# Step sizes on VectorE among the splits of X, a state-space product four pieces later in each head, meta tokens last in X, and q, k, v copied in destination order

## The chip, the cores and the metric

One core of a Trainium2 chip runs the whole layer in one launch. The metric is the device time of that launch in microseconds (us), from a run without the profiler; the trace comes from one further execution with it. PE is the matrix engine, PEld its weight loads, DVE the vector engine, ACT the scalar engine, POOL the general-purpose engine, SP the engine that issues most DMAs.

## The reference

The layer works on 16 meta tokens and 512 real tokens, 2048 channels wide, in float32. What is computed, cut to what matters here:

```python
proj = hf @ w_in                                  # 528 x 2048 by 2048 x 6144
u_ssm, g_ssm, q, k, v, g_sb = split(proj)         # each 1024 wide
# state-space branch: 64 groups of 16 channels, 64 complex states
dt = exp(log_dt); mag = exp(lam_re * dt); angle = lam_im * dt
h_t = (mag * e^{i angle}) * h_{t-1} + B u_t ;  y = Re(C h) + d * u
y_ssm = (GLU(gelu(y)) * silu(g_ssm)) @ w_branch_ssm
# stick-breaking attention, 8 heads of 128, strictly causal, scores q k / sqrt(128)
y_sb = (attention(q, k, v) * silu(g_sb)) @ w_branch_sb
gates = sigmoid(hf @ w_gate + b_gate)
out = layer_norm(ALPHA * hf + (gates_1 * y_ssm + gates_2 * y_sb) @ w_out)[16:]
```

## The kernel before, in words

Every float32 matrix product is done as three products of halves: an operand `a` is split into `ah` (rounded to the matrix engine's format by an ACT copy) and `al` (the rest, a DVE subtraction, `split_lo`, line 96), and `mm3` adds `ah*bh + ah*bl + al*bh`. The transposed input X is kept split in SBUF, `Xh` and `Xl`, as 16 chunks of 128 channels (`split_x`). The weights stream in from memory as 238 chunks of 128x1024 (`raw`), which ACT and DVE split into `whi` and `wlo` (`prep_upto`, line 126 and again line 96), three buffers each.

PE's work is cut into **pieces**. A unit of work is one output tile of 128 channels: 16 pieces, one for each chunk of X, 8 pieces for each weight chunk (a **slot**). `unit_real` multiplies the 512 real tokens (3 products of 512 columns in a piece), `unit_full` all 528 in two halves of 272 and 256 columns, `HALF` (6 products in a piece), `unit_pair`, used once at the start for u and v of head 0, two outputs at a time (12 products in a piece). A unit's result leaves the accumulator in a `fin_...` function at the start of the next slot.

The order of everything is the order in which the program is written: each engine takes its instructions in that order, and an instruction that waits holds up all behind it on its engine. Work beside the weight products is placed by hand: `schedule` takes pairs of a piece number and a function, counted from the piece at hand, and `run_fillers` calls each function just ahead of its piece. So a **step at piece 34** stands, on every engine that it uses, between the instructions of pieces 33 and 34.

The stages that the change touches:
- **Parameters** (start of the program, pieces 0 to 63). `params_a` computes the step sizes dt = exp(log_dt) and from them `mag` and `th`, on POOL; `params_v` (sine, cosine, exponential on DVE, in small steps), `params_g` (power tables on POOL) and `params_w` (further tables on DVE, ending in `pvt`, which `store_pv` writes to memory) follow. `steps(g, at, end, n)` spreads a generator's steps over the pieces from `at` to `end`.
- **Splits of X.** During the pair of units at the start, X's chunk c is split two pieces ahead of the piece that needs it.
- **Head stages** (`ssm_stages(i)` and `att_stages(i)`), which run while PE does the 80 weight pieces of the next head. In the state-space part, `s2` builds the tile `ot` on DVE, `s3` multiplies it with `bb` (8 small products, line 702), `s3b` takes the result out (ACT copy, DVE addition of `dd`, a DMA to `sd`), `s4` loads it back as `mt`, `s5` (line 731) starts the scan that `s7` ends. `s3` and `s5` write the same PSUM tile, aux2, of which there is one. In the attention part, `zblk` and `zb` make scores and a scan, `t01` and `t0` transpose the weights, `evb` splits the transposed tile (`ath` by ACT, `atl` by DVE), and `av(0)` at piece 37 multiplies them with the values `vh`, `vl`. `f3` of head 0 (six DVE operations, `ec` and `es`) stands at piece 46.

Meta tokens have columns 0 to 15 of X, real tokens 16 to 527. The real tokens are stored time step by time step (j) within blocks (k), so q, k and v are put into natural order by the copy that takes them out of PSUM.

Of the kernel before, what the change touches and what calls it, by code (L numbers as in the profile page):

```python
# [12 lines left out]
ALU = mybir.AluOpType  # L13
# [6 lines left out]
T = 8  # L20
NK = 66
MK = 2
L = T * NK
S = 512
SK = S // T
NM = T * MK
HALF = ((0, 272), (272, L))
LP = 576
NT = 8
NG = 8  # L30
# [8 lines left out]
def kernel(  # L39
# [49 lines left out]
    for kind, _ in MIX_ORDER:  # L89
        n_ = 4 if kind == "g" else 2  # L90
# [4 lines left out]
    def tt(out, a, b, op, eng=V):  # L95
        eng.tensor_tensor(out, a, b, op)  # L96

    def split_lo(lo, src, hi):
        tt(lo, src, hi.bitcast(F32), ALU.subtract)
# [31 lines left out]
    def mm3(o, ah, al, bh, bl, start, stop):  # L131
        PE.matmul(o, ah, bh, start=start, stop=False)  # L132
        PE.matmul(o, ah, bl, start=False, stop=False)  # L133
        PE.matmul(o, al, bh, start=False, stop=stop)  # L134
# [25 lines left out]
    def schedule(items):  # L160
        fillers.extend((piece[0] + p_, f) for p_, f in items)
        fillers.sort(key=lambda t: t[0])
# [20 lines left out]
    with tc.manual_schedule():  # L183
# [21 lines left out]
        def split_x(c):  # L205
            x, n = xts[c]
            r = x[:, 0, :].rearrange("p (j k) -> p j k", k=NK)[:, :, MK:NK]
            h, lo = jk(Xh[:, c, NM:L], SK), jk(Xl[:, c, NM:L], SK)
            A.copy(h, r)
            if n:  # L210
                m = x.rearrange("p c (j k) -> p c j k", k=NK)[:, :, :, 0:MK]
                mh_, ml_ = (t[:, c:c + n, 0:NM].rearrange("p c (j k) -> p c j k", k=MK) for t in (Xh, Xl))
                A.copy(mh_, m)
            split_lo(lo, r, h)
            if n:
                split_lo(ml_, m, mh_)
# [61 lines left out]
        def ts(o, a, s1, s2, op0, op1, e=V):  # L278
            e.tensor_scalar(o, a, s1, s2, op0, op1)
# [181 lines left out]
        zer = tp.tile([16, 112], F32, name="zer")  # L461

        def params_a():
            yield from vexp(dt, dt, G, "g")
            tt(mag, lr, dt, ALU.mult, G)
            tt(th, li, dt, ALU.mult, G)

        def params_v():

# [9 lines left out]
        def params_g():  # L479
            tt(mg8, mag[:, 0:64], mag[:, 0:64], ALU.mult, G)  # L480
            tt(mg8, mg8, mg8, ALU.mult, G)
            tt(mg8, mg8, mg8, ALU.mult, G)
            yield from params_e()
# [71 lines left out]
        def drain(g):  # L555
            for _ in g:
                pass
# [8 lines left out]
        def steps(g, at, end, n):  # L566
            def one_(g=g):
                next(g, None)
            return [(at + ((end - at) * k) // n, one_) for k in range(n)] + [(end, lambda: drain(g))]
# [4 lines left out]
        def store_pv():  # L574
            for src, dst in pvt_:
# [2 lines left out]
            [(18, lambda: [SP.dma_start(out=sd[i].rearrange("c (g t) -> c g t", t=240)[:, :, 0:112],  # L578
                                            in_=zer[:, None, :].to_broadcast([16, NG, 112]))
                           for i in range(NT)])]  # L580
            + [(2, lambda: drain(params_a())), (3, lambda: ts(maskl, masku, -1.0, 1.0, ALU.mult, ALU.add, G))]
            + steps(gv_, 19, 35, 40)
            + [(35, lambda: drain(params_g()))]
            + steps(gw_, 35, 60, 37)
            + [(61, store_pv)]
        )

        mp = None
# [61 lines left out]
        def ssm_stages(i):  # L650
# [143 lines left out]
                    in_=z.rearrange("p g k -> p (g k)"),  # L794
                )

            a = [(13, s1), (16, s1b), (20, s2(0)), (24, s2(1)), (26, s2(2)), (34, s3), (36, s3b), (39, s4)]
            if i == 0:
                a = [(24, s1), (27, s1b), (29, s2(0)), (31, s2(1)), (33, s2(2)), (37, s3), (39, s3b), (42, s4)]
            return [(0, s0)] + a + [  # L800
                (50, s5), (52, s5a), (55, s5b), (57, s5c), (66, s7), (69, s7b), (71, s8), (74, s9)]

# [152 lines left out]
        def unit_real(finish):  # L955
            a = new_acc()
            for half in range(2):
                def mk(kk, half=half):
                    def f(h, lo):
                        c = 8 * half + kk  # L960
                        ws = slice(kk * P, (kk + 1) * P)
                        mm3(a, h[:, ws], lo[:, ws], Xh[:, c, NM:L], Xl[:, c, NM:L],
                            c == 0, c == KT - 1)
                    return f
                slot([mk(kk) for kk in range(8)], (lambda: finish(a)) if half else None)


        def parts(t, aa):
            n = t[:, NM:L].rearrange("p (k j) -> p j k", j=T)
            yield n[:, 0:4, :], jk(aa[0][:, NM:272], SK)  # L970
            yield n[:, 4:8, :], jk(aa[1][:, 0:256], SK)
            yield t[:, 0:NM].rearrange("p (k j) -> p j k", j=T), jk(aa[0][:, 0:NM], MK)


        late = [lambda c=c: split_x(c) for c in range(1, KT)]
# [25 lines left out]
        for i in range(NT):  # L1001
            def fin_u(aa, i=i):
                u = ta("us", [P, L])
                uj = jk(u, NK)[:, ::-1, :]
                A.copy(uj[:, 0:4, MK:NK], jk(aa[0][:, NM:272], SK))
                A.copy(uj[:, 4:8, MK:NK], jk(aa[1][:, 0:256], SK))
                A.copy(uj[:, :, 0:MK], jk(aa[0][:, 0:NM], MK))
                A.dma_start(out=ud[i], in_=u)

            def fin_g(a, i=i):  # L1010
                t = ta("gsig", [P, S])
                A.activation(t, a, ACTF.Sigmoid)
                g_ = ta("gs", [P, S], F32, 2)
                tt(g_, a, t, ALU.mult)
                heads.setdefault(i, {})["gs"] = g_

            def fin_v(aa, i=i):
                v = ta("vT", [P, L])
                for d, a in parts(v, aa):
                    A.copy(d, a)  # L1020
                heads.setdefault(i, {})["vT"] = v

            def fin_k(aa, i=i):
                kh, kl = ta("kh", [P, L], F32R), ta("kl", [P, L], F32R)
                for (d, a), (l_, _) in zip(parts(kh, aa), parts(kl, aa)):
                    A.copy(d, a)
                    split_lo(l_, a, d)
                heads[i]["kh"], heads[i]["kl"] = kh, kl

            def fin_q(a, i=i):  # L1030
                qh, ql = ta("qh", [P, S], F32R), ta("ql", [P, S], F32R)
                A.copy(nat(qh), jk(a, SK))
                split_lo(nat(ql), jk(a, SK), nat(qh))
                heads[i]["qh"], heads[i]["ql"] = qh, ql

            if i == 0:
                unit_pair(fin_u, fin_v)
                unit_real(fin_g)
            else:
                unit_full(fin_u)  # L1040
                unit_real(fin_g)
                unit_full(fin_v)
            unit_full(fin_k)
            unit_real(fin_q)
            run_fillers()
            assert not fillers, fillers
            if i == 0:
                mb_st, at = open_main()
                f1, f2, f3 = ssm_load(0)
                schedule([(3, f2), (4, f1), (46, f3), (17, lambda: [V.tensor_copy(a[:, 4, 0:128], d0[:, 0:2, 0:64]) for a in at])])  # L1050
            schedule(ssm_stages(i) + att_stages(i))
            if i < NT - 1:
                f1, f2, f3 = ssm_load(i + 1)
                schedule([(45, f1), (61, f3), (72, f2)])


        def fin_gs(a, j):
# [206 lines left out]
        c = ctr[0]  # L1264
# [115 lines left out]
```

## Time and profile before

| what | us |
|---|---|
| time, median of 3 runs (1495.54 to 1496.41) | 1495.86 |
| time of the profiled execution | 1495.39 |
| its span, first to last instruction | 1493.6 |
| around the span in that execution (the difference) | 1.8 |
| PE busy with matmuls | 1454.4 (97%) |
| DVE busy | 764.9 (51%) |
| ACT busy | 421.3 (28%) |
| POOL busy | 68.6 (5%) |

Busy time is the sum of an engine's instruction durations with overlaps counted once. PE is close to full over the whole span, so what is left of the span is the time in which PE had nothing to do or ran at a lower granted clock. The trace names, for every instruction that found its engine idle, what released it.

### The profile page before, as it was taken

To read this page: it belongs to the slowest core of one execution; us is meant where nothing else is said; L and a number is where in the kernel's file an instruction comes from. 1 tells how busy PE (TensorE), PEld (TensorE's weight loads), DVE (VectorE), ACT (ScalarE), POOL (GpSimd) and SP (SyncE) were. 2 spreads that over 40 slices of the span, in tenths; PEclk is the share of its full clock that TensorE was granted. 3 is DMA by queue.
4 is the path that set the end of the run, shared out by engine and by line. 5 is a ranking of instruction groups with operands and counts; after the bars stand their busy time and mean duration, and the time that the engine had idled before them with its cause. 6 is when DMAs were issued, how large, how long until landed. Compare 5 with 4: busy or idle time off the path is not lost.

```text
span 1493.6 us, 19236 instructions
## 1 busy us (share of the span) xinstructions
PE 1454.4 (97%) x7888; PEld 1261.6 (84%) x7888; DVE 764.9 (51%) x1124; ACT 421.3 (28%) x640; POOL 68.6 (5%) x125
## 2 busy tenths in 40 slices
PE   8979999999999999999999999999999999999996
PEld 7879898989898989788888888888888888888885
DVE  6977767676766676644222222222444444423357
ACT  5322323232323232323222222222332222221120
POOL 6650000000000000000000000000000000000000
PEclk9999999999999999999999999999999999999998
DMA  7243443434343434345433333333444444374333
GB/s 272 71 134 89 128 102 122 115 120 115 109 116 107 129 99 132 100 115 174 141 117 119 117 120 127 120 127 120 148 150 148 155 141 149 134 204 149 98 99 113
DMA packets 94040, 191.99 MB, mean 129 GB/s; under 512 B 28160, under 2 KB 41728, under 8 KB 93184
## 3 DMA queue, kind: packets, MB, share of 16 engines
q1 hardware_dynamic: 75248, 172.87, 38.0%
q10 hardware_dynamic: 18704, 17.90, 3.6%
q8 instruction: 62, 1.02, 0.3%
q14 instruction: 26, 0.21, 0.0%
HBM read 168.45 MB, written 22.28 MB: 128 GB/s over the span
## 4 chain that ended last, share of the span: by engine, by line
PE 82%; DVE 13%; POOL 2%; issue 1%; ACT 1%; DMA 1%; SPq 0%; DVEq 0%; ACTq 0%; POOLq 0%
PE acc L132 23%; PE acc L133 23%; PE acc L134 23%; PE aux L132 3%; PE aux L133 2%; PE aux L134 2%; DVE wlo L96 2%; DVE Aall L866 2%; DVE ot L96 1%; ACT whi L126 1%; PE aux L770 1%; PE aux L731 1%; PE aux L766 1%; DVE tA L96 1%; DVE vt L96 1%
## 5 line engine op out<-in xcount | busy, mean ns | idle before, releaser
L96 DVE TENSOR_TENSOR wlo<-raw,whi 128x1024 fp32r<-128x1024 f32 (+1 forms) x242 | 294.4, 1218 | 610.0 <-ACT whi L126 607.2
L132 PE MATMUL acc<-Xh,whi 128*128 128x512 f32 (+2 forms) x1664 | 577.8, 347 | 7.9 <-ACT whi L231 4.5
L133 PE MATMUL acc<-Xl,whi 128*128 128x512 f32 (+2 forms) x1664 | 571.5, 343 | 0.4 <-DVE Xl L96 0.3
L134 PE MATMUL acc<-Xh,wlo 128*128 128x512 f32 (+2 forms) x1664 | 570.5, 343 | 0.7 <-DVE wlo L96 0.7
L126 ACT CAST whi<-raw 128x1024 fp32r<-128x1024 f32 x238 | 250.0, 1052 | 671.4 <-PE acc L133 519.7
L132 PEld LDWEIGHTS acc<-Xh,whi 128*128 128x128 f32 x1664 | 316.1, 190 | 43.6 <-ACT whi L231 4.5
L134 PEld LDWEIGHTS acc<-Xh,wlo 128*128 128x128 f32 x1664 | 315.3, 190 | 36.3 <-DVE wlo L96 1.0
L133 PEld LDWEIGHTS acc<-Xl,whi 128*128 128x128 f32 x1664 | 316.3, 190 | 34.5 <-DVE Xl L96 0.9
L134 PE MATMUL acc<-sh,wlo 128*128 128x512 f32 x128 | 49.8, 389 | 0.0
L134 PE MATMUL acc<-whi,ml 128*128 128x512 f32 x128 | 49.8, 389 | 0.0
L132 PE MATMUL aux<-whi,mh 128*128 128x512 f32 x128 | 49.8, 389 | 0.0
L132 PE MATMUL acc<-zh,whi 128*128 128x512 f32 x128 | 49.8, 389 | 0.0
L132 PE MATMUL acc<-sh,whi 128*128 128x512 f32 x128 | 49.8, 389 | 0.0
L134 PE MATMUL acc<-oh,wlo 128*128 128x512 f32 x128 | 49.8, 389 | 0.0
L133 PE MATMUL acc<-wlo,mh 128*128 128x512 f32 x128 | 49.8, 389 | 0.0
L134 PE MATMUL aux<-whi,ml 128*128 128x512 f32 x128 | 49.8, 389 | 0.0
L134 PE MATMUL acc<-zh,wlo 128*128 128x512 f32 x128 | 49.8, 389 | 0.0
L133 PE MATMUL acc<-ol,whi 128*128 128x512 f32 x128 | 49.8, 389 | 0.0
L133 PE MATMUL acc<-zl,whi 128*128 128x512 f32 x128 | 49.8, 389 | 0.0
L132 PE MATMUL acc<-whi,mh 128*128 128x512 f32 x128 | 49.8, 389 | 0.0
L133 PE MATMUL acc<-sl,whi 128*128 128x512 f32 x128 | 49.8, 389 | 0.0
L132 PE MATMUL acc<-oh,whi 128*128 128x512 f32 x128 | 49.8, 389 | 0.0
(239 smaller groups left out, 1513.5 us busy)
## 6 DMA issues: line engine op xcount, KB each, us to landing
raw<-wst SPq DMA_DIRECT2D x238, 512.0 KB
gtd<-gsg ACTq DMA_DIRECT2D x32, 256.0 KB
gt<-gtd SPq DMA_DIRECT2D x32, 256.0 KB
X<-brep SPq DMA_DIRECT2D x8, 512.0 KB
X<-pvd SPq DMA_DIRECT2D x16, 256.0 KB
X<-sd SPq DMA_DIRECT2D x8, 512.0 KB
xs<-xr SPq DMA_DIRECT2D x8, 512.0 KB
xt<-xT SPq DMA_DIRECT2D x7, 528.0 KB
```

Of the source, the lines that this page charges most:

```text
L96: eng.tensor_tensor(out, a, b, op)
L126: A.copy(h, t)
L132: PE.matmul(o, ah, bh, start=start, stop=False)
L133: PE.matmul(o, ah, bl, start=False, stop=False)
L134: PE.matmul(o, al, bh, start=False, stop=stop)
L731: PE.matmul(vp[:, g, 0:NK], W["vt"][:, g].rearrange("p r q -> p (r q)"), ut[:, g * NK:g * NK + NK], start=True, stop=True,)
L766: PE.matmul(yp[:, g, 0:SK], W["ot"][:, g].rearrange("p t c -> p (t c)"), hs[:, g * NK + MK - 1:g * NK + MK - 1 + SK], start=True, stop=False,)
L770: PE.matmul(yp[:, g, 0:SK], W["mt"][:, g, :], ut[:, g * NK + MK:g * NK + MK + SK], start=False, stop=True,)
L866: V.tensor_tensor_scan(ab[:, 0:n - 1][:, ::-1], kp[:, 1:n][:, ::-1], one.to_broadcast([P, n - 1]), 1.0, ALU.mult, ALU.mult,)
```

## The change

- `params_a` runs on VectorE in single steps, at pieces 3 to 10 among the splits of X, where before all of it was issued to POOL at piece 2. `params_v` moves from pieces 19-35 to 10-26, `params_g` from 35 to 26, `params_w` from 35-60 to 27-54, `store_pv` from 61 to 55.
- `s3` moves from piece 34 to 38 (head 0: 37 to 44), `s3b` from 36 to 40 (39 to 46), `s4` from 39 to 46 (42 to 52); `f1` of the next head from 45 to 54.
- X holds the real tokens in columns 0 to 511 and the meta tokens in 512 to 527; the two halves of a full unit are 256 and 272 columns.
- The copies and splits of q, k and v walk the destination in its own order and the PSUM source with a stride; before it was the other way round.

```diff
-HALF = ((0, 272), (272, L))
+HALF = ((0, 256), (256, L))
...
-            h, lo = jk(Xh[:, c, NM:L], SK), jk(Xl[:, c, NM:L], SK)
+            h, lo = jk(Xh[:, c, 0:S], SK), jk(Xl[:, c, 0:S], SK)
...
-                mh_, ml_ = (t[:, c:c + n, 0:NM].rearrange("p c (j k) -> p c j k", k=MK) for t in (Xh, Xl))
+                mh_, ml_ = (t[:, c:c + n, S:L].rearrange("p c (j k) -> p c j k", k=MK) for t in (Xh, Xl))
...
         def params_a():
-            yield from vexp(dt, dt, G, "g")
-            tt(mag, lr, dt, ALU.mult, G)
-            tt(th, li, dt, ALU.mult, G)
+            yield from vexp(dt, dt, V, "m")
+            tt(mag, lr, dt, ALU.mult)
+            tt(th, li, dt, ALU.mult)
+            yield
...
-            + [(2, lambda: drain(params_a())), (3, lambda: ts(maskl, masku, -1.0, 1.0, ALU.mult, ALU.add, G))]
-            + steps(gv_, 19, 35, 40)
-            + [(35, lambda: drain(params_g()))]
-            + steps(gw_, 35, 60, 37)
-            + [(61, store_pv)]
+            + steps(params_a(), 3, 10, 22)
+            + [(7, lambda: ts(maskl, masku, -1.0, 1.0, ALU.mult, ALU.add, G))]
+            + steps(gv_, 10, 26, 52)
+            + [(26, lambda: drain(params_g()))]
+            + steps(gw_, 27, 54, 37)
+            + [(55, store_pv)]
...
-            a = [(13, s1), (16, s1b), (20, s2(0)), (24, s2(1)), (26, s2(2)), (34, s3), (36, s3b), (39, s4)]
+            a = [(13, s1), (16, s1b), (20, s2(0)), (24, s2(1)), (26, s2(2)), (38, s3), (40, s3b), (46, s4)]
             if i == 0:
-                a = [(24, s1), (27, s1b), (29, s2(0)), (31, s2(1)), (33, s2(2)), (37, s3), (39, s3b), (42, s4)]
+                a = [(24, s1), (27, s1b), (29, s2(0)), (31, s2(1)), (33, s2(2)), (44, s3), (46, s3b), (52, s4)]
...
         def parts(t, aa):
-            n = t[:, NM:L].rearrange("p (k j) -> p j k", j=T)
-            yield n[:, 0:4, :], jk(aa[0][:, NM:272], SK)
-            yield n[:, 4:8, :], jk(aa[1][:, 0:256], SK)
-            yield t[:, 0:NM].rearrange("p (k j) -> p j k", j=T), jk(aa[0][:, 0:NM], MK)
+            n = t[:, NM:L].rearrange("p (k j) -> p k j", j=T)
+            kj = lambda ap, n_: ap.rearrange("p (j k) -> p k j", k=n_)
+            yield n[:, :, 0:4], kj(aa[0][:, 0:256], SK)
+            yield n[:, :, 4:8], kj(aa[1][:, 0:256], SK)
+            yield t[:, 0:NM].rearrange("p (k j) -> p k j", j=T), kj(aa[1][:, 256:272], MK)
...
             def fin_q(a, i=i):
                 qh, ql = ta("qh", [P, S], F32R), ta("ql", [P, S], F32R)
-                A.copy(nat(qh), jk(a, SK))
-                split_lo(nat(ql), jk(a, SK), nat(qh))
+                kj = lambda ap: ap.rearrange("p (k j) -> p k j", j=T)
+                ak = a.rearrange("p (j k) -> p k j", k=SK)
+                A.copy(kj(qh), ak)
+                split_lo(kj(ql), ak, kj(qh))
...
-                schedule([(45, f1), (61, f3), (72, f2)])
+                schedule([(54, f1), (61, f3), (72, f2)])
```

The first place is DVE during the pair of units at the start. Before, its rows there are only splits of X (`Xl`) and of weight chunks (`wlo`); here is what stands around the splits of chunks 8 and 9 before.

```order
L96 TENSOR_TENSOR wlo<-raw,whi 128x1024
L96 TENSOR_TENSOR Xl<-xt,Xh 128x512
L96 TENSOR_TENSOR Xl<-xt,Xh 128x2x16
L96 TENSOR_TENSOR wlo<-raw,whi 128x1024
L96 TENSOR_TENSOR Xl<-xt,Xh 128x512 x2
```

The same place after the change, with the small operations of `params_a` (tiles `ds` and `s`, 128x128) between them.

```order
L96 TENSOR_TENSOR wlo<-raw,whi 128x1024
L283 SCALAR_TENSOR_TENSOR ds_333<-ds_333,ds_314 128x128 x2
L279 TENSOR_SCALAR ds_377<-ds_311 128x128
L96 TENSOR_TENSOR Xl<-xt,Xh 128x512
L96 TENSOR_TENSOR Xl<-xt,Xh 128x2x16
L96 TENSOR_TENSOR wlo<-raw,whi 128x1024
L96 TENSOR_TENSOR ds_401<-ds_311,ds_377 128x128
L279 TENSOR_SCALAR ds_401<-ds_401 128x128
L279 TENSOR_SCALAR s_404<-ds_377 128x128
L96 TENSOR_TENSOR Xl<-xt,Xh 128x512
```

In all, 24 operations of `params_a` and the first 26 of `params_v` now stand ahead of the last split of X on DVE.

The second place is PE in the stages of head 1 (run during the weight pieces of head 2's u, g and v). Before, `s3` (line 702) stands three pieces ahead of `av(0)`; these are the rows around it.

```order
L133 MATMUL acc<-Xl,whi 128x256
L134 MATMUL acc<-Xh,wlo 128x256
L702 MATMUL aux_2141<-ot,bb 32x64 x8
L132 MATMUL acc<-Xh,whi 128x272
L133 MATMUL acc<-Xl,whi 128x272
L134 MATMUL acc<-Xh,wlo 128x272
```

After the change, the last products of `av(0)` (`ath`, `atl`), one weight piece, and then `s3` (now line 704).

```order
L132 MATMUL aux<-ath,vh 128x256
L133 MATMUL aux<-atl,vh 128x256
L134 MATMUL aux<-ath,vl 128x256
L132 MATMUL acc<-Xh,whi 128x256
L133 MATMUL acc<-Xl,whi 128x256
L134 MATMUL acc<-Xh,wlo 128x256
L132 MATMUL acc<-Xh,whi 128x272
L133 MATMUL acc<-Xl,whi 128x272
L134 MATMUL acc<-Xh,wlo 128x272
L704 MATMUL aux_2161<-ot,bb 32x64 x8
```

`s3` has changed places with `av(0)` on PE; the order on DVE of what the two wait for (`ot`, then the splits `atl`) is the same before and after.

The third place is DVE in the stages of head 0, where `X_1460<-aux_1429,dd` (numbers tell buffers of one name apart) is `s3b`'s addition, which reads `s3`'s result. Before, it follows directly on the splits for `av(0)`.

```order
L96 TENSOR_TENSOR ot<-ot,X_1363 128x1024
L96 TENSOR_TENSOR atl<-aux,ath 16x256 x2
L96 TENSOR_TENSOR X_1460<-aux_1429,dd 32x8x16
L96 TENSOR_TENSOR wlo<-raw,whi 128x1024
L96 TENSOR_TENSOR gsig<-aux,gs 128x8x32
```

After the change it stands behind `f3`'s six operations, whose last ones are the first rows here.

```order
L96 TENSOR_TENSOR ec<-tA,tB 128x576
L96 TENSOR_TENSOR tA<-ear,ebi 128x576
L96 TENSOR_TENSOR tB<-eai,ebr 128x576
L96 TENSOR_TENSOR es<-tA,tB 128x576
L96 TENSOR_TENSOR X_1517<-aux_1475,dd 32x8x16
L96 TENSOR_TENSOR atl<-aux,ath 128x256
```

`s5` on PE, at piece 50, writes the tile that this addition reads.

## Rows read from the trace of the kernel before

**Rows 1.** From the page: busy us, share of the span and number of instructions of each engine; and POOL's busy share, in tenths, in 40 slices of 37.3 us.
```profile
PE 1454.4 (97%) x7888; PEld 1261.6 (84%) x7888; DVE 764.9 (51%) x1124; ACT 421.3 (28%) x640; POOL 68.6 (5%) x125
...
POOL 6650000000000000000000000000000000000000
```

**Rows 2.** The waits of PE: the waiting line, what released it, us in total, times, longest.
```profile
PE aux L702 <- DVE ot L96: 15.5, 8, 6.3
...
PE aux L849 <- DVE vl L96: 1.9, 1, 1.9
```

**Rows 3.** PE in five stretches: the stretch and its length, PE busy us (instructions), granted clock as a share of full speed, DMA share, GB/s.
```profile
66.80:80.50 13.70, 8.83 (x55) 0.88 0.45 116
80.50:84.60 4.10, 4.10 (x21) 0.58 1.01 267
111.90:118.60 6.70, 6.67 (x37) 0.50 0.19 64
120.00:124.00 4.00, 4.00 (x36) 1.00 0.72 145
183.90:185.40 1.50, 0.23 (x3) 1.00 0.93 314
```

**Rows 4.** PE in order of time at piece 15, the last of the pair of units: its second product, the first that reads `Xl`.
```profile
30.56 0.29 PE L133 MATMUL acc<-Xl,whi 128*128 128x272 f32 x1
```

**Rows 5.** DVE in order of time, 10 to 33 us: start, us, engine, line, operation, tiles, count, and the idle time before it with its releaser. Runs of `Xl` hold splits of 512 columns and small ones of the meta columns (in the first row four and two).
```profile
10.55 2.92 DVE L96 TENSOR_TENSOR Xl<-xt,Xh 128x512 fp32r<-128x512 f32 x6
...
17.84 0.98 DVE L96 TENSOR_TENSOR Xl<-xt,Xh 128x512 fp32r<-128x512 f32 x2 [1.07 <-ACT Xh L209]
...
32.32 1.23 DVE L96 TENSOR_TENSOR wlo<-raw,whi 128x1024 fp32r<-128x1024 f32 x1 [3.26 <-ACT whi L126]
```

**Rows 6.** DVE in order of time in the stages of head 1: a weight split, an operation behind it, and two 512-wide ones behind each other.
```profile
163.99 1.22 DVE L96 TENSOR_TENSOR wlo<-raw,whi 128x1024 fp32r<-128x1024 f32 x1 [2.66 <-ACT whi L126]
165.14 0.28 DVE L96 TENSOR_TENSOR kp<-kp,masku 128x128 f32<-128x128 f32 x1
...
166.36 0.69 DVE L96 TENSOR_TENSOR tA<-X,X 128x512 f32<-128x512 f32 x1
166.96 0.69 DVE L96 TENSOR_TENSOR tB<-X,X 128x512 f32<-128x512 f32 x1
```

**Rows 7.** DVE in order of time: the first operation of `params_v`, the weight split behind its 26th operation, and further on two operations of which the second reads the first's result.
```profile
36.38 0.31 DVE L279 TENSOR_SCALAR ds<-th 128x128 f32<-128x128 f32 x1 [2.83 <-POOL th L96]
...
41.20 1.21 DVE L96 TENSOR_TENSOR wlo<-raw,whi 128x1024 fp32r<-128x1024 f32 x1
...
46.41 0.29 DVE L96 TENSOR_TENSOR ds<-ds 128x128 f32<-128x128 f32 x1
46.74 0.29 DVE L283 SCALAR_TENSOR_TENSOR ds<-ds,ds 128x128 f32<-128x128 f32 x1
```

**Rows 8.** In order of time, where head 0's units end: ACT's copy of a table from the parameters (`be`), DVE's last parameter operation, SP's two writes of `pvt`, ACT's copy of the values.
```profile
65.43 0.63 ACT L517 ACTIVATE be<-pwi 128x512 f32<-128x512 f32 x1 [1.47 <-DVE pwi L96]
...
72.71 0.68 DVE L96 TENSOR_TENSOR pvt<-cmv 64x512 f32<-64x512 f32 x1
74.93 1.32 SPq L576 DMA_DIRECT2D pvd<-pvt  x2
79.11 0.73 ACT L816 CAST vh<-aux 128x512 fp32r<-128x512 f32 x2 [5.91 <-DMA pvd<-pvt]
```

**Rows 9.** Head 0 in order of time: a scan of the scores and the splits for `av(0)` on DVE; `s3` on PE.
```profile
93.41 1.41 DVE L866 TENSOR_TENSOR_SCAN Aall<-kp,one 128x399 f32<-128x399 f32 x1
111.80 0.74 DVE L96 TENSOR_TENSOR atl<-aux,ath 16x256 fp32r<-16x256 f32 x2
111.93 1.91 PE L702 MATMUL aux<-ot,bb 128*32 128x64 f32 x16 [6.33 <-DVE ot L96]
```

**Rows 10.** Head 0 in order of time: `s3b`'s addition and the last operation of `f3` on DVE, and `s5` on PE.
```profile
114.42 0.28 DVE L96 TENSOR_TENSOR X<-aux,dd 32x128 f32<-32x128 f32 x1 [1.89 <-ACT X L712]
128.56 0.76 DVE L96 TENSOR_TENSOR es<-tA,tB 128x576 f32<-128x576 f32 x1
127.59 1.67 PE L731 MATMUL aux<-ut,vt 128*128 128x66 f32 x14
```

**Rows 11.** Head 1 in order of time: an ACT copy of scores, the same scan as in rows 9, the splits for `av(0)`; then PE's `s3` and the second product of `av(0)`, the first that reads `atl`.
```profile
172.15 0.51 ACT L854 ACTIVATE sg<-aux 128x400 f32<-128x400 f32 x1 [2.21 <-DVE Aall L96]
176.41 0.99 DVE L866 TENSOR_TENSOR_SCAN Aall<-kp,one 128x399 f32<-128x399 f32 x1
187.47 0.73 DVE L96 TENSOR_TENSOR atl<-aux,ath 16x256 fp32r<-16x256 f32 x2
185.34 1.08 PE L702 MATMUL aux<-ot,bb 128*32 128x64 f32 x16 [1.27 <-DVE ot L96]
188.97 0.28 PE L133 MATMUL aux<-atl,vh 16*128 16x256 f32 x1
```

**Rows 12.** Head 7: `s3` on PE, ACT's copy for `av(0)` and what held it, the second product of `av(0)`.
```profile
622.61 1.08 PE L702 MATMUL aux<-ot,bb 128*32 128x64 f32 x16 [1.50 <-DVE ot L96]
625.22 0.62 ACT L816 CAST ath<-aux 16x256 fp32r<-16x256 f32 x2 [4.58 <-DVE us L96]
626.35 0.38 PE L133 MATMUL aux<-atl,vh 16*128 16x256 f32 x1
```

**Rows 13.** ACT's copies of q out of PSUM: count, busy us, mean ns of one, idle time before them.
```profile
L1032 ACT CAST qh<-acc 128x512 fp32r<-128x512 f32 x8 | 9.3, 1157 | 0.0
```

More of the change, by code (lines that the diff above doesn't have):

```diff
@@ L961, in f @@
                         ws = slice(kk * P, (kk + 1) * P)
-                        mm3(a, h[:, ws], lo[:, ws], Xh[:, c, NM:L], Xl[:, c, NM:L],
+                        mm3(a, h[:, ws], lo[:, ws], Xh[:, c, 0:S], Xl[:, c, 0:S],
                             c == 0, c == KT - 1)
@@ L1004, in fin_u @@
                 uj = jk(u, NK)[:, ::-1, :]
-                A.copy(uj[:, 0:4, MK:NK], jk(aa[0][:, NM:272], SK))
+                A.copy(uj[:, 0:4, MK:NK], jk(aa[0][:, 0:256], SK))
                 A.copy(uj[:, 4:8, MK:NK], jk(aa[1][:, 0:256], SK))
-                A.copy(uj[:, :, 0:MK], jk(aa[0][:, 0:NM], MK))
+                A.copy(uj[:, :, 0:MK], jk(aa[1][:, 256:272], MK))
                 A.dma_start(out=ud[i], in_=u)
```

## The prediction

> **What bounds the kernel now.** I read the engine totals first: PE is busy for 97% of the span, DVE for half of it [rows 1]. So the time changes only where PE stands idle or runs at a lower clock, and work on another engine counts only where PE waits for it. I take three costs of PE's before from the rows.
>
> The list of PE's waits comes next. Every head makes PE wait once in `s3` (line 702) for DVE's `ot`: 15.5 us in eight waits, of which head 0 has 6.3 [rows 2]. Another 1.9 falls on line 849, which wants the split values `vl`.
>
> Then the stretches. Between 66.8 and 80.5 PE is busy 8.83 of 13.70 us, so it idles 4.87 [rows 3], all of it in four stalls while the last tables of head 0 are made. The clock falls after it: 0.58 from 80.5 to 84.6. It falls again after the 6.3 us wait in head 0: 37 instructions take 6.67 us at a clock of 0.50, and 36 take 4.00 a little later at 1.00. After head 1's short wait it is still 1.00.
>
> **A, the pair of units at the start: loses 4.0.** 24 operations of `params_a`, on POOL before, and the first 26 of `params_v`, which began at 36.38 [rows 7], now stand ahead of the last split of X. PE wanted that split at 30.56 [rows 4]. I add up DVE's work from the point where the first small one stands, 12.9 (the end of the first run, 10.55 + 2.92, less one split of 0.60, since one of that run now stands behind) [rows 5].
> - A 512-wide operation: 166.36 to 166.96, 0.60 [rows 6]. 11 splits of X: 6.6.
> - A meta split: (2.92 - 4 x 0.60) / 2 = 0.26 [rows 5]. Five: 1.3.
> - A weight split: 163.99 to 165.14, 1.15 [rows 6]. Three: 3.45.
> - 26 operations of `params_v`: 36.38 to 41.20, 4.8, or 0.185 each [rows 7].
> - 24 of `params_a`: the same pitch gives 4.4. But this exponential is one chain. About eight stand directly behind the operation that they read, and such a neighbour starts 0.33 behind it (46.41 to 46.74) [rows 7]; 8 x 0.15 is 1.2 more. I take 5.6.
>
> The last split ends at 12.9 + 21.75 = 34.6, 4.0 after PE's need. DVE had idle time in this stretch, as 1.07 at 17.84 [rows 5], but it now arrives later than the data, so none is left to cover anything. Bounds: all 50 at 0.185 give 2.8; all at 0.33 give 16.5 us for them, and PE is 10 late.
>
> [...]
>
> **B, the stretch 66.8 to 80.5: gains 8.2.** The chain of tables moves ahead: `params_w` ends at piece 54 instead of 60 and `store_pv` stands at 55 instead of 61. A full piece lasts 0.735 us, so this is 6 x 0.735 = 4.4 us earlier against PE. Before, ACT stood in `be`, waiting for DVE's `pwi` [rows 8], with a weight copy behind it; the longest stall was the 1.9 [rows 2], where `pvt` leaves DVE at 72.71, its DMA goes out at 74.93 and ACT copies `vh` at 79.11 only after it (5.91 idle) [rows 8]. Each stall is shorter than 4.4, so I let all four go. That is 4.87 idle, plus 0.16 refill of PE at each (0.6), plus the clock: 4.1 us at 0.58 lose 1.7, and 8.83 at a mean of 0.88 lose 1.0 [rows 3]. Sum 8.2. PE's lateness from A does not change this, for DVE's later work waits for PE's weight chunks. Bounds: nothing (the same stalls further on) and 8.2.
>
> **C, head 0 at `s3`: gains 1.0.** `s3` waits for `ot` until 111.93, and PE would now first come to `av(0)`, whose splits `atl` stand right behind `ot` on DVE, at 111.80 [rows 9]. So the wait goes from `s3` to `av(0)`, and what releases it is late by the same DVE queue. What shrinks is the queue: a scan takes 1.41 here and 0.99 in head 1 [rows 9, 11], while POOL is half busy up to about 110 us [rows 1], and POOL's chain now starts nine pieces earlier. I put this at 1.0, from 0 to 3.3.
>
> **D, head 0 at `s5`: loses 0.9.** `s3b`'s addition now stands behind `f3`, whose last operation starts at 128.56 and ends at 129.3 [rows 10]. With the addition's 0.28 it is done near 129.6. `s5` writes the tile that it reads; PE came to it at 127.59 [rows 10], and with `s3`'s 1.1 now in between comes at 128.7. It waits 0.9 (0 to 2).
>
> **E, heads 1 to 6: gains 0.5.** Here too the wait moves. PE would reach the second product of `av(0)` at 188.97 - 1.27 - 1.08 = 186.6, and the first `atl` is ready half way through a pair that starts at 187.47, at 187.9 [rows 11]. It waits 1.25 instead of the 1.27 + refill. Nothing makes `atl` earlier: DVE and ACT release each other in a chain (172.15) [rows 11] and DVE stood waiting at 163.99 [rows 6]. I give 0.08 a head, from 0 to 1.3.
>
> **F, head 7: loses 1.0.** ACT's copy for `av(0)` is held until 625.22 by the `us` chain, whatever `s3` does, and the second product of `av(0)` stays at 626.35 [rows 12]. `s3`'s 1.08 was done in time that PE now spends waiting, and comes after.
>
> **The rest: nothing.** The copies of q last 1.16 us [rows 13] and may shorten; ACT is busy 28% [rows 1] and waits for PE ahead of most of its work, so the gain falls into its idle time. Without that cover a copy would cost its 1.16. The order of X's columns gives the same matmuls.
>
> **Sum.** -4.0 + 8.2 + 1.0 - 0.9 + 0.5 - 1.0 = 3.8 gained. The profiled execution took 1495.39, its span and 1.8 around it; the median of the runs is 1495.86, 0.5 more. From the median: **1492.1**.
>
> **The rivals.**
> 1. Head 0 catches up too. If the earlier parameters also free DVE before 111.8, C gives its bound of 3.3 and the low clock after it goes in part (2.3 us more of C): 1492.1 - 3.5 = 1488.6. For it: the scan's 1.41. Against: DVE stood waiting at the start of head 0 as well as in head 1. 16%.
> 2. `s3`'s wait vanishes in heads 1 to 6 (6 x 1.35 = 8.1, 7.6 beyond E), with some of rival 1: about 1482. Against: `atl` stands directly behind `ot`. 6%.
> 3. The early stalls go only in part: if half of B stays, 1492.1 + 4.1 = 1496.2, no change. For it: ACT's table copies now stand ahead of another weight copy, and PE also runs ahead by what it no longer loses. 16%.
> 4. Slower: the small operations pay their full length, 0.29 each and more. 50 x 0.29 = 14.5, so the last split ends at 12.9 + 11.35 + 14.5 = 38.8, 8.2 late instead of 4.0: 1496.3. PE then waits at piece after piece, and if its clock falls as it did after 66.8 to 80.5, 1.7 to 2.7 more are lost: 1498.0 to 1499.0 and beyond. It is slower from a lateness of about 11 us, by waits or by clock. 12%.
>
> **How the numbers follow.** The forecast has 50%, with 1489.5 to 1494.5 as its own range. What a measurement can tell is 0.2%, 3.0 us: faster is below 1492.9, slower above 1498.9. The forecast is close to that border; I count 30 of its 50 as faster. With rivals 1 and 2 that is 0.52; the other 20 with rival 3 are 0.36; rival 4 is 0.12. The range 1486.5 to 1497.5 leaves out rival 2 and most of rival 4.
>
> **What would show it.** A: line 133's first product of piece 15 near 34.5, released by DVE's `Xl`; right at 33.4 to 35.5, wrong where there is no wait or it is past 38. B: no PE idle time above 0.3 in the last 14 us before head 0's scores and a clock near 1.00 there; wrong if line 849 still waits for `vl`. C, E: line 132 or 133 with `ath`, `atl` in the list of waits, with about the sum that line 702 had; wrong if both are gone. D: a wait of `s5` for the addition `dd`. F: `s3` of head 7 directly behind `av(0)`, no shorter in all. The prediction falls most easily by B, which is the largest term, and by the pitch in A.

## The result, and the profile after

The changed kernel takes **1513.36 us** (median, 1513.31 to 1513.99), the kernel before, beside it, 1495.70: the ratio is 1.0119, with a 95% interval of 1.0102 to 1.0137. It is 17.7 us slower, where 1492.1 was forecast and 1497.5 was the end of the range.

The engine totals after (answering to [rows 1]), and PE's waits (answering to [rows 2]; the waiting line, its releaser, us in total, times, longest):

```profile
PE 1474.3 (98%) x7888; PEld 1263.4 (84%) x7888; DVE 759.6 (50%) x1145; ACT 408.7 (27%) x640; POOL 49.0 (3%) x95
```
```profile
PE aux L133 <- DVE atl L96: 11.4, 7, 3.7
PE acc L132 <- ACT whi L231: 4.6, 1, 4.6
PE aux L132 <- DVE atl L96: 2.6, 1, 2.6
PE aux L132 <- ACT ath L818: 2.4, 1, 2.4
PE acc L133 <- DVE Xl L96: 1.9, 3, 1.2
...
PE aux L733 <- DVE X L96: 0.5, 1, 0.5
```

The list of waits looks much as forecast. `s3` has none left and `av(0)` has them all (11.4 + 2.6 + 2.4, where `s3` had 15.5), and `s5` waits 0.5 for `dd`. But PE is *busy* 20 us longer with the same 7888 products. So the loss is not in waiting: the products themselves got slower. Where, two kinds of anchor show, the first score product (line 849 before, 851 after) and `s5` (731 and 733). These are rows of single lines, first of before, then of after: min, median and max duration in ns, and the start of the first (head 0) and of the last one (head 7).

```profile
L849 PE MATMUL aux<-kh,qh x40: 281/284/388, 80.5 to 610.1; 128*128 128x264 f32 x16, 128*128 128x256 f32 x8, 128*128 128x272 f32 x8, 128*128 128x400 f32 x8
L731 PE MATMUL aux<-ut,vt x128: 218/275/276, 127.6 to 639.0; 128*128 128x66 f32 x128
```
```profile
L851 PE MATMUL aux<-kh,qh x40: 281/284/348, 76.1 to 612.3; 128*128 128x264 f32 x16, 128*128 128x256 f32 x8, 128*128 128x272 f32 x8, 128*128 128x400 f32 x8
L733 PE MATMUL aux<-ut,vt x128: 219/275/325, 122.4 to 645.0; 128*128 128x66 f32 x128
```

At head 0's first score the changed kernel is 4.4 us ahead (80.5 to 76.1), at head 0's `s5` 5.2, which answers to terms A to D (4.3 forecast). At head 7's scores it is 2.2 behind, at head 7's `s5` 6.0, and at the end of the span 18.0 (1493.6 to 1511.6). So 7.4 were lost over heads 1 to 6, 3.8 in head 7, and 12.0 behind the heads, where the change moves no step at all.

**Behind the heads** stand only 512-column products. The groups of one of the three products between 700 and 1000 us, before and then after (count | busy, mean ns of one), and under each all engines in that stretch (PE busy and count first):

```profile
L132 PE MATMUL acc<-Xh,whi 128*128 128x512 f32 x442 | 171.9, 389 | 0.0
```
```profile
700.00:1000.00 300.00, 300.00 (x1325) 248.52 (x1324) 70.69 (x59) 75.78 (x85) 0.00 (x0) 1.00 0.38 125
```
```profile
L132 PE MATMUL acc<-Xh,whi 128*128 128x512 f32 x429 | 169.7, 396 | 0.0
```
```profile
700.00:1000.00 300.00, 300.00 (x1288) 241.70 (x1287) 70.71 (x60) 75.45 (x86) 0.00 (x0) 1.00 0.38 121
```

At a clock of 1.00 in both, without a wait, a product comes every 300 / 1325 = 226.4 ns before and every 300 / 1288 = 232.9 ns after. Behind head 7's `s5` stand 1770 such products on X; at 6.5 ns each they make 11.5 of the 12.0 us.

**In the heads** the clock is the difference. Stretches of the changed kernel, the length, busy us (count) of PE, PEld, DVE, ACT, POOL, granted clock, DMA share, GB/s: where the stalls of [rows 3] were, then behind the waits of heads 1, 2, 3, 4, 5, 6 and 7; above them head 1's wait.

```profile
182.80 0.38 PE L133 MATMUL aux<-atl,vh 16*128 16x256 f32 x1 [1.28 <-DVE atl L96]
```
```profile
62.00:76.00 14.00, 14.00 (x87) 12.43 (x86) 10.77 (x16) 4.16 (x9) 13.14 (x20) 1.00 0.54 154
...
184.00:188.00 4.00, 4.00 (x29) 3.63 (x29) 0.00 (x0) 0.00 (x0) 0.00 (x0) 0.59 0.17 65
...
258.50:262.50 4.00, 4.00 (x29) 3.58 (x28) 0.00 (x0) 0.00 (x0) 0.00 (x0) 0.57 0.17 67
...
333.00:337.00 4.00, 4.00 (x42) 3.76 (x41) 0.00 (x0) 0.46 (x1) 0.00 (x0) 1.00 0.19 71
...
405.70:409.00 3.30, 3.30 (x23) 3.05 (x22) 0.00 (x0) 0.00 (x0) 0.00 (x0) 0.51 0.25 94
480.00:484.00 4.00, 4.00 (x29) 3.58 (x30) 0.00 (x0) 0.00 (x0) 0.00 (x0) 0.60 0.28 110
553.00:559.00 6.00, 5.08 (x46) 4.70 (x47) 1.19 (x3) 0.39 (x1) 0.00 (x0) 1.00 0.28 90
627.00:634.40 7.40, 6.62 (x30) 5.09 (x31) 0.74 (x2) 0.62 (x2) 0.00 (x0) 0.54 0.39 106
```

The kernel before, behind head 1's wait at `s3` (the stretch in [rows 3] ends where that wait ends, at 185.40):

```profile
185.40:189.40 4.00, 4.00 (x38) 3.64 (x38) 3.00 (x7) 0.75 (x2) 0.00 (x0) 1.00 0.38 118
```

Behind an equally long wait (1.28, before 1.27) PE now runs some 3.4 us at a granted clock of 0.50 in heads 1, 2, 4 and 5 (183.88 to 187.29 in head 1), and twice as long in head 7 (627.61 to 634.44). From one wait at `av(0)` to the next it is 74.5 us with such a stretch and 73.0 without, so each costs 1.5 us. Heads 3 and 6 show none behind the same 1.28 us, and there the change costs next to nothing (72.9 before).

### The profile page after: what moved, and what is told of

It is laid out like the page before. It is cut to its first block, busy times and chain, and to the rows that moved or that the text cites. A ratio compares the mean times of both kernels' runs of the same rounds, so it can differ in the third digit from the quotient of the medians.

```text
span 1511.6 us, 19239 instructions
## 1 busy us (share of the span) xinstructions
PE 1474.3 (98%) x7888; PEld 1263.4 (84%) x7888; DVE 759.6 (50%) x1145; ACT 408.7 (27%) x640; POOL 49.0 (3%) x95
## 4 chain that ended last, share of the span: by engine, by line
PE 58%; DVE 0%; DVEq 0%; issue 0%
PE acc L132 17%; PE acc L134 17%; PE acc L133 17%; PE aux L132 2%; PE aux L133 2%; PE aux L134 2%; DVE xs L1235 0%; DVE xs L1238 0%; PE aux L704 0%; PE aux L772 0%; PE aux L733 0%; PE aux L768 0%; PE aux L879 0%; DVEq L1381 0%; DVE bs L1215 0%; DVE xs L1212 0%
## 5 line engine op out<-in xcount | busy, mean ns | idle before, releaser
L133 PE MATMUL aux<-wlo,mh 128*128 128x512 f32 x128 | 49.8, 389 | 0.0
```

## The experiments

Times are medians; each ratio stands against the kernel before, run on the same chip in the same session (1495.2 to 1495.9).

### The address of X

In the program both kernels hold `Xh` from byte 55360 of each partition, a pad of 48 columns ahead of it. The real tokens started 64 bytes on, at 55424; with the meta tokens last they start at 55360. The weight buffers `whi` and `wlo` start at 30592 and then every 4096 bytes, all with a remainder of 128 by 256, as 55424 has. Four kernels move the start of the real tokens:

```diff
-        xp.tile([P, 48], F32, name="xpad")
+        xp.tile([P, 32], F32, name="xpad")      # 64 in the fourth
```

> The changed kernel with the 48 pad columns ahead of X cut to 32, so that column 0 of X starts 64 bytes further down and every chunk's real tokens start on a multiple of 256 bytes again. In the changed kernel a 512-column product on X starts every 233.3 ns, before every 226.6 ns; the new layout moved its first column by 64 bytes. Theory 1, start address: the products go back to 227 ns, and the 2,600 or so of them give back 6.7 ns each, 17 us: about 1496. Theory 2, the order of the columns itself or DVE's and ACT's accesses to X: they stay at 233 ns and the time at 1513.

> The changed kernel with the meta tokens back in columns 0 to 15 and the halves of 272 and 256 columns; step sizes, the moved product and the copies as changed. Both theories: 512-column products at 227 ns, about 1496 to 1497. Together with the run with the pad cut it tells apart address and column order.

> The kernel before with the same pad cut from 48 to 32 columns, nothing else. Its real tokens then start 64 bytes off, as in the changed kernel. Theory 1: its 512-column products go from 227 to 233 ns, 17 us slower, about 1512. Theory 2: no change, 1496.

> The changed kernel with 64 pad columns ahead of X instead of 48, so that column 0 stands at 55424, the byte address in a partition at which the real tokens stood before (128 more than a multiple of 256). At 55360 and at 55296 (64 more, and a multiple of 256) the 512-column products started 233 ns apart, at 55424 227. Theory 1, the start address: 227 ns with the new column order too, some 12 us less than the changed kernel: 1501. Theory 2, the column order itself: 233 ns, 1512.

Measured: 1511.26 (ratio 1.0105) for the pad of 32, 1501.84 (1.0044) for meta tokens first, **1507.65 (1.0084, 1.0069 to 1.0099) for the kernel before with the pad of 32**, and 1500.36 (1.0026, 1.0015 to 1.0037) for the pad of 64. The product of the same stretch in these four, in this order:

```profile
L132 PE MATMUL acc<-Xh,whi 128*128 128x512 f32 x429 | 169.5, 395 | 0.0
```
```profile
L132 PE MATMUL acc<-Xh,whi 128*128 128x512 f32 x442 | 171.9, 389 | 0.0
```
```profile
L132 PE MATMUL acc<-Xh,whi 128*128 128x512 f32 x429 | 169.7, 396 | 0.0
```
```profile
L132 PE MATMUL acc<-Xh,whi 128*128 128x512 f32 x442 | 171.9, 389 | 0.0
```

So the column order is innocent: with the new order at the old address (55424) the product takes 389 ns, and the old order at 55360 takes 396. The first expectation was wrong in its rule, though. A multiple of 256 (55296, the pad of 32) is slow too, so what matters is not a round address. Two others were off in size: meta tokens first came out 5 us above 1496 to 1497, since the low clock of the heads is still in it, and the pad of 32 cost the kernel before 12.5 us where 17 was expected. What matters about the start, the next run shows: it moves the weight buffers and X together.

```diff
+    padl = ctx.enter_context(tc.tile_pool(name="padl", bufs=1))
+    padl.tile([P, 32], F32, name="leftpad")
     raw_p = ctx.enter_context(tc.tile_pool(name="raw", bufs=3))
```

> The kernel before with a pad of 128 bytes ahead of the weight buffers, which moves the weight buffers and X by 128 bytes together; the tiles zh and sh of later stages stay. Theory 1a, the start counts against that of the weights that PE loads at the same time (both have the same remainder by 256 in the kernel before): X stays at 227 ns, the products with zh and sh go to 233: a few us slower. Theory 1b, the start counts by itself: X goes to 233 ns, zh stays at 227: about 1507.

1502.31 (1.0040, 1.0025 to 1.0055). Two groups of later stages in it, which before had 389 both, and the group with X (line numbers two higher than before):

```profile
L134 PE MATMUL acc<-oh,whi 128*128 128x512 f32 x128 | 49.8, 389 | 0.0
...
L134 PE MATMUL acc<-zh,whi 128*128 128x512 f32 x124 | 49.0, 395 | 0.0
```
```profile
L134 PE MATMUL acc<-Xh,whi 128*128 128x512 f32 x441 | 171.5, 389 | 0.0
```

`Xh` and `oh`, which moved with the weights, stay at 389; `zh`, which stayed where it was, goes to 395. Theory 1a holds: the start of the streamed operand counts against that of the weights that PE loads beside it. Remainders by 256 that are equal give 389 ns; differences of 64 and of 128 both give 395 or 396. A difference of 256 cost nothing: X's chunks lie 2304 bytes apart (9 times 256), so counted by 512 every second chunk differs from the weights by 256, and the others by 0; behind the heads the products of all 16 come every 226.7 ns in the kernel before.

The rule is one for 512 columns. The six products of a full piece (256 and 272 columns; start to start at full clock, the mean of some 465 in each trace) took 738 ns in the kernel before (differences of 0 and 64 for its two halves), 733 with both at 0 (the pad of 64), 738 with both at 128 (the changed kernel with the pad of 32), but 725 with both at 64, in the changed kernel. Its 384 full pieces so gain 4.9 us, and the 768 products of 512 columns that run beside the heads lose 5.0. So the address cost its 12 us behind the heads only: from head 0's `s5` to head 7's it is 522.6 us in the changed kernel and 522.3 with the pad of 64, with the low clock in the same heads.

### The moved product, alone and taken back

```diff
-(26, s2(2)), (34, s3), (36, s3b), (39, s4)]        # heads 1 to 7
+(26, s2(2)), (38, s3), (40, s3b), (46, s4)]
-(33, s2(2)), (37, s3), (39, s3b), (42, s4)]        # head 0
+(33, s2(2)), (44, s3), (46, s3b), (52, s4)]
-schedule([(45, f1), ...                            # f1 of the next head
+schedule([(54, f1), ...
```

> The changed kernel with the pad cut to 32, and s3, s3b, s4 and f1 back at their old pieces (34, 36, 39, 45; head 0 37, 39, 42). In the changed kernel PE's clock is at 0.5 for 3.4 us behind the wait in heads 1, 2, 4 and 5 and 6.8 us in head 7, which it was in none of them before. Theory 1 (the moved product brings the low clock: the wait at av(0) is followed at once by av(0) and s3, before by three full pieces): no low clock in heads 1 to 7, 8 to 11 us faster than the run with the pad cut alone, about 1487. Theory 2 (the earlier parameters or the copies bring it): the low clock stays, no gain beyond 1 us.

> The kernel before with only s3, s3b, s4 and f1 at the later pieces of the change. Theory 1, the moved product alone brings the low clock after the waits at av(0): stretches at 0.5 behind most of the waits of heads 1 to 7, 7 to 11 us slower, 1502 to 1506. Theory 2, it takes the earlier parameters too: no low clock, within 2 us of 1495.

Taken back (with the pad of 32; the diff read the other way): 1504.20 against 1511.26 without that, 7.1 less, somewhat under the 8 to 11 expected, and no low clock in heads 1 to 7. With the pad of 32 alone it was in heads 2, 3, 4 and 7, behind waits of 1.13 to 1.17 us in heads 2 to 4. Alone, on the kernel before: **1508.42 (1.0085, 1.0068 to 1.0101), 12.5 slower**, a little beyond what was expected. In the trace five heads (2, 4, 5, 6, 7; the first two here) show what heads 1 and 2 show above:

```profile
263.00:267.00 4.00, 4.00 (x29) 3.61 (x28) 0.00 (x0) 0.00 (x0) 0.00 (x0) 0.57 0.08 31
410.00:414.00 4.00, 4.00 (x29) 3.69 (x28) 0.00 (x0) 0.00 (x0) 0.00 (x0) 0.58 0.26 97
```

### The parameters alone, and the copies alone

> The kernel before with only the parameters as in the change (step sizes on VectorE, all later steps earlier). Terms A, B and C of the prediction alone: PE 2.8 late at the last split of X (as measured in the changed kernel), no stalls between 66 and 80 us, no low clock before head 0's wait: 5 to 6 us faster, 1489 to 1490. If the clock of heads 1 to 7 hung on the parameters: 1495 or more.

> The kernel before with only the copies and splits of q, k and v in destination order. The prediction has them hidden: 1495.9 less 0 to 1. If they count where DVE and ACT hand over to each other in the scores, the waits of s3 in heads 1 to 7 get shorter: up to 7 x 1.3, 1487.

The parameters alone: **1489.67 (0.9957, 0.9942 to 0.9972), 6.2 faster**, as expected; `s3` keeps its eight waits (15.7 us), the clock its 1.00 in heads 1 to 7. The copies alone: 1495.45 (0.9998, 0.9989 to 1.0007), nothing, although one copy of `qh` fell from 1157 ns [rows 13] to 580 in the changed kernel. The parts add up: -6.2 + 12.5 - 0.4, and 12.5 for the address (from the kernel before with the pad of 32), are 18.4; the whole change measured 17.7.

### What brings the low clock

Five kernels on the wait itself. The first two move `s3` away from `av(0)` (pieces 43 and 44, heads 1 to 7); of the first only the time is used.

> The changed kernel with X at its old address (64 pad columns) and, in heads 1 to 7, s3 at piece 43 instead of 38 (s3b 45, s4 48), so that six pieces lie between av(0), where PE waits, and s3, instead of one. Theory 1, the low clock comes where the wait, av(0) and s3 stand close together: no low clock in heads 1 to 6, 1492 to 1494. Theory 2, the wait ahead of av(0) is enough, wherever s3 stands: the low clock stays, 1500.

> The changed kernel with X at its old address and s3 of heads 1 to 7 at piece 44 (s3b 46, s4 48), for the trace that the run with s3 at 43 didn't leave. That run's time (1500.8 against 1500.4 with s3 at 38) says that the distance of s3 from the wait doesn't matter. Theory 2 (the wait ahead of av(0) is enough): 1500 to 1501, and stretches at 0.5 behind the waits of most of heads 1 to 7. Theory 1 (closeness of s3): none of them.

1500.78 and 1499.93, against 1500.36 with `s3` at 38. The low clock is still there behind five of the seven waits (heads 1, 3, 4, 6, 7; here head 1, and head 2, which stays at 1.00), with `s3` six pieces later than in the change:

```profile
183.50:187.50 4.00, 4.00 (x23) 4.00 (x22) 0.00 (x0) 0.28 (x1) 0.00 (x0) 0.57 0.12 47
257.00:261.00 4.00, 4.00 (x33) 3.87 (x33) 0.05 (x1) 0.70 (x1) 0.00 (x0) 1.00 0.35 122
```

So `s3`'s nearness is not the cause. Then the length of the wait, at `av(0)` and at `s3`:

```diff
-keys = [(0, 2), (1, 1), (2, 4)] if hb == 0 ...
+keys = [(1, 1), (2, 4), (0, 2)] if hb == 0 ...
```

> The changed kernel with X at its old address and, in av(0), the products of the 16 meta keys last instead of first (three products with atl of 16 rows, which comes last from DVE, behind six of 128 rows). Everything that waits and its order on DVE stay. The first of the three now stands six products, some 0.8 us, later, so the wait of heads 1 to 7 shrinks from 1.3 to about 0.5. If the clock falls because of the length of that wait, no low clock in heads 1 to 6: 1500.4 less 6 x 0.8 and less 5 x 1.7, about 1487. If position alone brings it: 1495.

> The changed kernel with X at its old address, the meta keys last in av(0), and av(0) of heads 1 to 7 at piece 36, so that the wait for the 16-row atl is about 1.4 long again (0.68 at piece 37) but stands behind the six 128-row products instead of ahead of them. Theory 1, the length of the wait decides: the low clock is back in several of heads 1 to 6, 1495 to 1500. Theory 2, it is what follows the wait directly (nine small products) that decides: no low clock, 1488 to 1490.

> The kernel before with s3 of heads 1 to 7 one piece earlier, at 33. PE then waits there 0.74 longer, some 2.0 instead of 1.27, and what follows stays. Nothing else changes, so the time is 1496 if the clock stays (PE is only idle earlier, and s3's end hangs on ot). Theory 1, the clock falls with the length of the wait: stretches at 0.5 in several heads, 1500 to 1508. Theory 2, a wait at s3 doesn't bring the low clock, only one at av(0): 1496.

With the 16-row products last, the wait of head 1, and the stretch from there on, are

```profile
181.45 0.38 PE L133 MATMUL aux<-atl,vh 16*128 16x256 f32 x1 [0.68 <-DVE atl L96]
```
```profile
181.00:185.00 4.00, 3.55 (x33) 3.18 (x34) 0.72 (x3) 0.00 (x0) 0.00 (x0) 1.00 0.40 135
```

and no head from 1 to 6 falls to the low clock: 1488.64 (0.9947, 0.9933 to 0.9962), 11.7 less than the same kernel with them first, for three products written behind six others. One piece earlier, with two waits of 0.48 and 0.71 two us apart instead of the one of 1.4 that was planned, the low clock is back in heads 1 and 5 (head 7 has it in both): 1494.76 (1.0007, 0.9990 to 1.0024). Head 1 there:

```profile
181.00:185.00 4.00, 4.00 (x29) 3.66 (x28) 0.00 (x0) 0.00 (x0) 0.00 (x0) 0.57 0.27 93
```

How many heads fall differs between executions of one kernel: the eight of this one took 1493.0 to 1499.9 us at mean granted clocks of 0.992 to 0.987, and a trace shows one execution. And the kernel before with `s3` one piece earlier, at 33: **1509.84 (1.0098, 1.0069 to 1.0127), 14 slower for one piece number**. Its wait in head 1, and the stretches behind those of heads 1 and 2; heads 3 to 7 all show 0.57 too:

```profile
185.25 0.91 PE L702 MATMUL aux<-ot,bb 128*32 128x64 f32 x13 [2.02 <-DVE ot L96]
```
```profile
186.50:190.50 4.00, 4.00 (x22) 4.00 (x22) 1.81 (x5) 0.97 (x2) 0.00 (x0) 0.57 0.45 141
261.70:265.70 4.00, 4.00 (x22) 4.00 (x22) 1.77 (x5) 0.92 (x2) 0.00 (x0) 0.57 0.44 142
```

The expectation was wrong that the longer wait alone costs nothing. The piece that PE did ahead of `s3` now comes behind it, so the 0.75 more of waiting is lost in every head: of the 15.4 us that the span is longer, 5.4 are waits at `s3` (20.9 instead of 15.5) and 10.3 PE's busy time (1464.7 instead of 1454.4), which is the clock.

A longer wait at the same place brings the low clock: at `s3` waits of 1.06 to 1.50 in none of 42 heads (heads 1 to 7 in six traces with `s3` ahead of `av(0)`), those of 2.01 to 2.19 in all seven; at `av(0)`, in heads 1 to 6, waits of 1.13 to 1.40 in 24 of 36 (six traces); with the 16-row products last, 0.67 to 0.68 in none of six, and 0.48 with 0.71 in two of six. The length does not decide alone, since heads with the same 1.28 differ, and that is left open. That the border lies lower at `av(0)` than at `s3` is shown; why is not. The 16-row products around it are a guess that no run separates.

### The wait taken away

If PE waits because it comes too early, it can come later. All on the kernel before with the early parameters: `s3` at 36 in heads 1 to 7 and `av(0)` at 40 in all; then also head 0's `s3` at 44 and its attention from `av(0)` on six pieces later; then that with lighter or denser parameter steps.

> The kernel before with the early parameters alone, and in all heads the consumers of late tiles moved past the wait: s3 from 34 to 36 (heads 1 to 7), av(0) from 37 to 40, avb(0) 42, t23a and its splits one piece later. If the wait of heads 1 to 7 is only a matter of when PE comes to ot and atl, it goes and nothing takes its place: 7 x 1.3 to 1.5, 9 to 10 us below the early parameters alone, 1479 to 1481. If the waits move to another consumer: 1489.

> As the run before, and in head 0 s3 at piece 44 instead of 37 (s3b 46, s4 52, f3 47, f1 54) and the second half of the attention six pieces later, so that the 6.6 us wait of head 0 and the low clock behind it go. Expected: 6 wait and up to 5 of clock, 1470 to 1474, if the weight splits that stand behind ot on DVE are early enough; if they are not, PE waits for wlo instead and the time stays near 1480.

> As the run before, with params_v at pieces 16 to 29 instead of 10 to 26 (params_g 29, params_w 30 to 55, store 56), so that only params_a stands among the splits of X. Term A by itself: PE was 2.7 late with 50 small operations ahead of the last split; with about 24 it should be late by less than 0.5, 2 us less than the run before. If the later tables bring back the stalls of 66 to 80 us, no gain.

> The fastest so far (early parameters, the consumers of late tiles past their waits in all heads, 1472.0) with params_v beginning at piece 12 instead of 10 and ending at 26 as before, and in head 0 s3 two pieces later (46, s3b 48, f3 49, s5 51). Term A: with about 20 small operations less ahead of the last split PE should be late by 0 to 1 instead of 2.7; the 1.4 wait of head 0's s3 goes. 1468 to 1470; above 1472 if DVE's denser work from piece 12 to 26 makes its weight splits late.

Measured: 1478.78 (0.9887, 0.9872 to 0.9901), 1472.03 (0.9841, 0.9826 to 0.9855), 1475.70 (0.9865, 0.9848 to 0.9881) and **1471.06 (0.9834, 0.9818 to 0.9851)**. The first takes away the waits of heads 1 to 7 and leaves head 0's; the second leaves 1.4 of that:

```profile
PE aux L704 <- DVE ot L96: 6.1, 1, 6.1
```
```profile
PE aux L704 <- DVE ot L96: 1.4, 1, 1.4
```

The lighter start fails as its second clause said. PE's first product behind the pair starts 1.4 us earlier than in the run before (34.49 against 35.87), still 1.6 later than in the kernel before, where less than 0.5 was expected. The tables of head 0 come later too, and the stalls of [rows 3] are back, with the low clock behind them:

```profile
PE acc L134 <- DVE wlo L96: 1.6, 2, 1.0
PE acc L132 <- ACT whi L126: 1.6, 1, 1.6
...
PE acc L132 <- DVE kl L96: 0.8, 1, 0.8
```

The last kernel starts `params_v` later but ends it at piece 26, and has head 0's `s3` at 46. It misses its 1468 to 1470 by 1 us and is hardly told from the second (1.0 us apart, on two chips). Behind the first wait for weights its longest is 1.0, and it is 24.8 us faster than the kernel before and 42.3 faster than the changed one.

## Why the prediction was wrong

- **The step that failed first** is "The order of X's columns gives the same matmuls". It looked at sizes and instructions, which are the same, and not at where the operand starts. The term was put at nothing and measured 12 to 13 us, nearly all of it behind the heads. No rival had it.
- **The step that failed second** is the pricing of E and F by waiting alone. The waits came out as worked out: "It waits 1.25" (measured 1.28), no gain in `atl`, the sum near 15.5 (16.4). But "After head 1's short wait it is still 1.00" was read from a stretch that ends with the wait, and it holds for a wait of 1.27 at `s3`; the prediction took this for a property of short waits. Moved to `av(0)`, the same length costs 1.5 us of clock in four of six heads. E was +0.5 and measured -7.4 over heads 1 to 6 (6.0 of it clock), F was -1.0 and measured -3.8. Rival 4 had the right kind of mechanism, a low clock behind more waiting, but in the pair of units, where the clock stayed at 1.00.
- **A** was put at -4.0 and measured -2.8: PE's first product behind the pair starts at 35.66 instead of 32.89, the lower bound of the term; with the parameters alone at 35.85, 3.0 late. DVE's last split ends at 33.4 instead of 34.6: a split with its meta columns takes 0.71 (15.41 to 16.12) where I had 0.60 + 0.26, and the operations of `params_a` together some 5.0 where I had 5.6. They are 21 and not 24, as DVE's instructions show (1145 against 1124): 0.24 each, where 5.6 for 24 makes 0.23. Rows of after, DVE in order of time:

```profile
15.41 0.79 DVE L96 TENSOR_TENSOR Xl<-xt,Xh 128x512 fp32r<-128x512 f32 x2
16.12 0.94 DVE L283 SCALAR_TENSOR_TENSOR ds<-ds,ds 128x128 f32<-128x128 f32 x3
...
32.73 0.70 DVE L96 TENSOR_TENSOR Xl<-xt,Xh 128x512 fp32r<-128x512 f32 x1
```

PE's first product behind the pair before; then, after, PE's longest wait in the pair, line 133's first product of piece 15 (at 33.49, inside the 33.4 to 35.5 that were named as a sign) and the first behind the pair:

```profile
32.89 0.50 PE L132 MATMUL acc<-Xh,whi 128*128 128x512 f32 x1 [0.84 <-ACT us L1006]
```
```profile
31.64 0.39 PE L133 MATMUL acc<-Xl,whi 128*128 128x256 f32 x1 [1.22 <-DVE Xl L96]
...
33.49 0.38 PE L133 MATMUL acc<-Xl,whi 128*128 128x256 f32 x1
...
35.66 0.51 PE L132 MATMUL acc<-Xh,whi 128*128 128x512 f32 x1 [0.55 <-ACT us L1008]
```

- **B** held, 8.2 forecast, and came out a little beyond its upper bound. With the parameters alone PE reaches its wait at head 0's `s3` at 99.6 instead of 105.6, 6.0 earlier, after being 3.0 late, so B is 9.0. In the changed kernel the stretch from 62 to 76 us has no idle time. For the 0.16 of refill at each stall no row was named; a product's time beyond the step to the next one is as much (389 less 226 ns, behind the heads in the kernel before).
- **C** was put at 1.0 and is nothing: with the parameters alone `s3` of head 0 still waits 6.6 us, and the 6.3 of before were no shorter by POOL's leaving. **D** was 0.9 and measured 0.5. That the 5.2 us at head 0's `s5` came near the 4.3 forecast is partly luck: A, B and D were better than forecast and made up for C.
- **The copies** held: nothing.

## What to carry over

A tile's base address was worth some 12 us here: before a change of layout, compare, for products of 512 columns, the remainder by 256 of the streamed operand's start with that of the weights (389 ns a product here where they are equal, 395 or 396 where they differ by 64 or 128), and read the mean duration of one product after it. A wait of PE is priced with the clock behind it, and here that price jumped: a wait that cost only its length at `s3` (1.27 us) cost more than double at `av(0)` (1.28, and 1.5 of clock in four of six heads), so let PE come later where the order allows it. Where two steps change places in front of one late tile, look for a third place in which nobody waits at all.

## What the runs showed of the hardware

- Between 700 and 1000 us of seven traces a 512-column float32 product on X came every 226.2 to 226.4 ns where the streamed operand and the weights start at the same remainder by 256 (four kernels), and every 232.9 to 233.1 ns where they differ by 64 or 128 (three). In the later stages of the kernel with the weights and X moved by 128 bytes one lasted 389 ns with `oh` (equal) and 395 with `zh` (128 apart). The products of 256 and 272 columns didn't follow this: six took 733 ns with both halves at 0 and 725 with both at 64.
- PE's granted clock fell to 0.50 for some 3.4 us behind waits of 1.13 to 1.40 us at `av(0)` in 24 of 36 heads, of 2.01 to 2.19 at `s3` in all seven, and behind two of 0.48 and 0.71 close together in two of six, but not behind 0.68 at `av(0)`, nor behind 1.06 to 1.50 at `s3`.
